# Routing of a mixture-of-experts layer: six tiles of 96 tokens, a scale for each token, and rows added into DRAM by accumulating DMAs

## The chip, the core and the metric

The kernel runs on one core of a Trainium2 chip. The time is that of the device, in microseconds, for one execution of the whole program. Runs before and after are compared by their median. Five engines work side by side: PE (TensorE, matmuls), DVE (VectorE), ACT (ScalarE), POOL (GpSimd) and SP (SyncE, which here only issues DMAs).

## The reference

One inference step of a decoder of two layers on 576 tokens (512 of a new sequence, 64 of eight others) with 1024 channels. Each layer has a mixer of three branches (S5, attention over a paged cache, Mamba-2) with an output projection w_o. Layer 0 goes on with a dense SwiGLU, layer 1 with eight experts, of which each token uses two. Around the end of layer 1's mixer, where the change lies, it computes:

```python
x = layer_norm(ALPHA * x + m, ln1_g[1], ln1_b[1])        # m: mixer's output, behind w_o
logits = x @ w_router + b_router                          # 576 x 8
top_val, top_idx = lax.top_k(logits, 2)
top_w = softmax(top_val)
f = sum over e of gate[:, e] * (silu(x @ w_gate[e]) * (x @ w_up[e])) @ w_down[e]
x = layer_norm(ALPHA * x + f, ln2_g[1], ln2_b[1])
```

## The kernel before

Activations lie with channels on the 128 partitions and tokens along the free axis, in eight blocks of channels, and tokens in two halves of 288 (`HF`, `h` = 0 and 1). Matmuls run with 32-bit operands that are split into a high and a low part: each weight block (512 KB, loaded by SP in `wload`, L265) is split into `wh` by ACT (L97) and `wl` by DVE (L106) in `wsplit`; three matmuls (L294 to L296) make one product. TensorE runs through weight block after weight block, and the splits are made some blocks ahead.

At the end of layer 1's mixer, `mixer_out` does for each half eight w_o blocks, each followed by an addition of the residual, and then the layer norm in `Norm.finish`: subtract the mean (L1466), squares on ACT (L1468), sums over channels by matmuls with a matrix of ones (L1470), router logits by matmuls of 8 output rows (L1479, tile `lgp`), root (L1481), a reciprocal 288 wide on all partitions (L1482), product with it, then gain and bias on ACT (L1494). With half 0 this lies beside half 1's w_o; with half 1 nothing is left for TensorE to do beside it.

`route` comes once, after half 1, for all 576 tokens in five tiles of 128 (the last 64): logits are transposed to tokens on partitions, the two largest are found, counted (matmuls L1693 to L1695 give each token's position in its expert), and ten matmuls with one-hot rows (`rsel`, L1712 and L1713) turn positions into the list of tokens of each expert's 176 slots (`tl`). Beside it `route_half` transposes the normalised rows and writes them to a DRAM tensor `X1D` by DMAs on ACT's queue (L1661; half 0's also to `X1C`, L1663). The weights of tokens are written to a DRAM table `WT` (L1751, L1752). `overflow` then loads the largest count into registers of all engines and branches (L1862, L1863); its body, for more than 176 tokens in one expert, isn't entered in the runs shown.

The expert loop gathers each expert's rows from `X1D` by two indirect DMAs on POOL (`gather`, L1762 and L1764), transposes and splits them (`tokens`, tile `xe`), runs gate, up and down blocks (`mm2`, L1788 to L1791; silu at L1809), and adds the result rows into `X1C` by two accumulating indirect DMAs (L1854). The slot weights come from `WT` by two indirect gathers for each expert, 16 in all (`slot_weights`, L1757, tile `rsw`).

Elsewhere, `gather_logs` (L972) issues 16 indirect gathers into `lfp` for each layer from POOL at the start of the program; `fox_sample` copies them out (L1001). The tile has two buffers.

Engines take their instructions in program order, and the framework puts in waits where tiles or DRAM tensors depend on each other; `tc.issue_after` orders instructions of one engine.

Of the kernel before, what the change touches and what calls it, by code (L numbers as in the profile page):

```python
# [36 lines left out]
FLAG, SLAG, ZLAG = 3, 1, 1  # L37
NPRE, NPS, NPP = 5, 2, 1
# [7 lines left out]
def decoder_step(ctx, tc, A, O):  # L46
# [79 lines left out]
    def dexp(out, x, n):  # L126
        ki_ = wk.tile([P, 80], I32, name="eki", bufs=1)
        f = wk.tile([P, 3, 80], F32, name="ef", bufs=1)
        k_, a_, r_, p_ = ki_[:, :n], f[:, 0, :n], f[:, 1, :n], f[:, 2, :n]
# [62 lines left out]
    tokid = consts.tile([P, 5], I32, name="tokid")  # L192
    pool.iota(tokid, pattern=[[P, 5]], base=0, channel_multiplier=1)
# [37 lines left out]
    def tr(out, in_, n):  # L231
        pe.transpose(out, in_, ident[:n, :n])  # L232
# [1200 lines left out]
    class Norm:  # L1433
# [19 lines left out]
        def finish(self, pr, g0, b0, ecol, out, mid=None):  # L1453
            R, h = self.R, self.h
            late = mid and h
# [9 lines left out]
            for j in range(8):  # L1465
# [3 lines left out]
                if h:  # L1469
                    last_ = pe.matmul(pv[:, :HF], lhsT=ones, rhs=sq, start=(j == 0), stop=(j == 7))  # L1470
# [6 lines left out]
            with tc.issue_after(last_.ins) if late else nullcontext():  # L1477
                for j in range(8 if mid else 0):
                    pe.matmul(lo_, lhsT=M["wr"][:, j], rhs=R(j), start=(j == 0), stop=(j == 7))  # L1479
# [3 lines left out]
            if mid:  # L1483
                mid(h, lo_, rs)
            for j in range(8):
                if late and j % 2:
                    M["pl"] = mul(pool, R(j), R(j), rs)
                else:
                    mul(dve, R(j), R(j), rs)
                g_, b_ = pr[:, g0 + j:g0 + j + 1], pr[:, b0 + j:b0 + j + 1]  # L1490
                if h and j % 2 and not late:
# [3 lines left out]
                out(j, h, R(j))  # L1495

# [3 lines left out]
    def mixer_out(l, mhl, out, done):  # L1500
# [4 lines left out]
        for h in range(2):  # L1505
# [3 lines left out]
            for j in range(8):  # L1509
# [4 lines left out]
                nrm.ready(j)  # L1514
            nrm.finish(prm[l], R_L1G, R_L1B, 1, out, done and done[0])
            if done:
                done[1](r, h)
# [59 lines left out]
    MB = dict(C=8, M=8, W=2, L=2, RW=2, XS=3, SQ=3, GT=6)  # L1577
# [31 lines left out]
    WT = dr.tile([T * NE, 1], F32, name="WT")  # L1609
# [4 lines left out]
    def route_init():  # L1614
        M["wr"] = U("RW", [P, 8, 8], F32, name="rtw")
        pool.dma_start(out=M["wr"], in_=A["moe_w_router"][0].rearrange("(k p) e -> p k e", p=P))
# [3 lines left out]
        M["rows"] = consts.tile([P, 2, 2, 5], I32, name="rrow")  # L1620
        M["wts"] = consts.tile([P, 2, 2, 5], F32, name="rwt")
# [6 lines left out]
        M["tw"] = consts.tile([P, 2, 8], I32, name="rtw8")  # L1628
        M["sw"] = consts.tile([P, 2, 8], F32, name="rsw")
        M["io"] = io = U("W", [P, CAP], F32, name="io")  # L1630
# [4 lines left out]
    def route_prep():  # L1635
        wb = U("RW", [P, 8, 8], F32, name="rtb")
        mul(dve, wb, M["wr"], bc(prm[1][:, R_L1B:R_L1B + 8], 2, 8))
        mul(dve, M["wr"], M["wr"], bc(prm[1][:, R_L1G:R_L1G + 8], 2, 8))
# [3 lines left out]
        add(dve, M["brt"], M["brt"], pt[:, 0:8])  # L1642

    def route_mid(h, o, rs):
        if not h:
            M["lg"] = wk.tile([P, T], F32, name="lg", tag="xp", bufs=4)
        mul(dve, M["lg"][:8, HS[h]], o, rs[:8])
        if h:
            route()

    def route_half(r, h):
        for i in ((0, 1), (2, 3, 4))[h]:
            n = P if i < 4 else 64
            t_ = U("C", [P, D], name="x1t")
            for j0 in (0, 4):
                pt = PF()
                for j in range(4):
                    k = j0 + j
                    tr(pt[:n, j * P:(j + 1) * P], r[k // 2][:, k % 2, i * P:i * P + n], P)
                M["x1"] = cp(t_[:n, j0 * P:j0 * P + 512], pt[:n])  # L1660
            act.dma_start(out=X1D[i * P:i * P + n], in_=t_[:n])  # L1661
            if h == 0:
                act.dma_start(out=X1C[i * P:i * P + n], in_=t_[:n])  # L1663

    def route():
        sc = U("C", [P, 640], name="rsc")
        pt = PX()
        L = sc[:, 0:40].rearrange("p (a b) -> p a b", a=5)
        dve.memset(L, 0.0)
        for i in range(5):  # L1670
            n = P if i < 4 else 64
            tr(pt[:n, i * 8:(i + 1) * 8], M["lg"][:8, i * P:i * P + n], 8)
        add(dve, L[:, 0:4], pt[:, 0:32].rearrange("p (i e) -> p i e", i=4), bc(M["brt"], 1, 4))
        add(dve, L[:64, 4], pt[:64, 32:40], M["brt"][:64])
        mx = sc[:, 40:80].rearrange("p (a b) -> p a b", a=5)
        ix = sc[:, 80:120].bitcast(U32).rearrange("p (a b) -> p a b", a=5)
        for i in range(5):
            dve.max(mx[:, i], L[:, i])
            dve.max_index(ix[:, i], mx[:, i], L[:, i])
        ef = sc[:, 120:130].rearrange("p (a b) -> p a b", a=2)  # L1680
        dve.tensor_copy(ef, ix[:, :, 0:2].rearrange("p i c -> p c i"))
        oh = sc[:, 130:210].rearrange("p (a b c) -> p a b c", a=2, b=5)
        for c in range(2):
            dve.tensor_tensor(oh[:, c], bc(e8f, 1, 5), bc(ef[:, c], 2, 8), op=OP.is_equal)
            dve.memset(oh[64:, c, 4], 0.0)
        cnt = sc[:, 210:250].rearrange("p (a b) -> p a b", a=5)
        add(dve, cnt, oh[:, 0], oh[:, 1])
        ls = sc[:, 250:298].rearrange("p (a b) -> p a b", a=6)
        dve.memset(ls[:, 0], 0.0)
        for i in range(5):  # L1690
            add(dve, ls[:, i + 1], ls[:, i], cnt[:, i])
        pt = PX()
        pe.matmul(pt[:, :40], lhsT=bef, rhs=cnt, start=True, stop=False)  # L1693
        pe.matmul(pt[:, :40], lhsT=ones, rhs=ls[:, 0:5], start=False, stop=True)
        pe.matmul(pt[:, 64:72], lhsT=ones, rhs=ls[:, 5], start=True, stop=True)  # L1695
        tmp = sc[:, 298:378].rearrange("p (a b c) -> p a b c", a=2, b=5)
        rp = sc[:, 378:388].rearrange("p (a b) -> p a b", a=2)
        for c in range(2):
            mul(dve, tmp[:, c], pt[:, :40].rearrange("p (i e) -> p i e", i=5), oh[:, c])
        dve.tensor_reduce(rp.rearrange("p c i -> p (c i)"), tmp.rearrange("p c i e -> p (c i) e"), axis=AX.X, op=OP.add)  # L1700
        oht = U("W", [P, 2, 5, 8], F32R, name="oht")
        tokf = sc[:, 420:425]
        dve.tensor_scalar(tokf, tokid, 1.0, None, op0=OP.add)
        for c in range(2):
            mul(dve, oht[:, c], oh[:, c], bc(tokf, 2, 8))
        io = M["io"]
        pl = PX()
        n_ = 0
        for c in range(2):
            for i in range(5):  # L1710
                s_ = wk.tile([P, CAP], F32R, name="rsel", tag="h288", bufs=4)
                (dve, dve)[i % 2].tensor_scalar(s_, io, rp[:, c, i:i + 1], None, op0=OP.is_equal)  # L1712
                pe.matmul(pl[:8, 0:CAP], lhsT=oht[:, c, i], rhs=s_, start=(n_ == 0), stop=(n_ == 9))  # L1713
                n_ += 1
        ps_ = sc[:8, 440:440 + CAP]
        dve.tensor_copy(ps_, pl[:8, 0:CAP])
# [321 lines left out]
```

## Time and profile before

| what | value |
|---|---|
| timed runs | 2384.43, 2384.25, 2366.11 us |
| median | 2384.25 us |
| profiled execution, its own time | 2400.34 us |
| its span in the trace | 2398.7 us |
| PE busy | 2277.4 us (95%) |
| DVE, ACT, POOL busy | 66%, 47%, 23% |
| mean granted clock of TensorE | 0.968 of full speed |

The span is the trace's first to last instruction; 1.6 us lie around it. Busy time is what instructions of an engine cover; a high share says that the engine bounds the kernel on the whole, not in each stretch. In the rows below a start is in microseconds from the start of the span, the number in brackets is the idle time ahead of the instruction, and behind the arrow stands what ended it ("issue": nothing that the profile shows).

### The profile page before, as it was taken

What the parts mean: (1) busy time and instruction counts of PE and PEld (TensorE: products, weight loads), DVE (VectorE), ACT (ScalarE), POOL (GpSimd) and SP (SyncE); (2) the same over time, 40 slices, a digit from 0 to 9 for tenths busy, and PEclk for the clock granted to TensorE, in tenths of its full rate; (3) what the DMA queues carried; (4) which work ended last, traced back from release to release, by engine and by line L of the source; (5) the groups of instructions that cost most, each with busy time, mean ns of one, the idle gap of its engine ahead of it and who ended that gap; (6) DMA issues with size and microseconds to landing.
All of it is one profiled execution on the core that took longest, in us unless ns stands there. A gap on an engine that the chain in (4) does not pass through costs nothing. (4 is left out here: it accounts for less than half of the span.)

```text
span 2398.7 us, 45369 instructions
## 1 busy us (share of the span) xinstructions
PE 2277.4 (95%) x17037; PEld 2158.2 (90%) x17038; DVE 1573.7 (66%) x3725; ACT 1134.5 (47%) x2538; POOL 560.4 (23%) x712
## 2 busy tenths in 40 slices
PE   5999999998999999999999999899999699999995
PEld 5899997888998999999899998789999599999995
DVE  4956687556588843334765697456447578888886
ACT  2354443453346323223644443354334467777773
POOL 6733224333130110001124324233003310101000
PEclk7999999999999999999999999899999799999997
DMA  5566556856445432233576557757333799999993
GB/s 125 174 177 206 160 155 186 202 160 215 118 126 157 147 96 83 80 89 103 139 188 184 157 152 195 186 156 211 89 99 108 199 229 255 255 253 259 236 258 100
DMA packets 587436, 399.91 MB, mean 167 GB/s; under 512 B 59436, under 2 KB 548188, under 8 KB 587176
## 3 DMA queue, kind: packets, MB, share of 16 engines
q1 hardware_dynamic: 475272, 236.30, 37.2%
q0 software_dynamic: 30912, 95.12, 14.4%
q10 hardware_dynamic: 81024, 65.51, 9.5%
q8 instruction: 136, 2.23, 0.4%
q14 instruction: 92, 0.75, 0.1%
HBM read 326.02 MB, written 70.92 MB: 165 GB/s over the span
## 5 line engine op out<-in xcount | busy, mean ns | idle before, releaser
L106 DVE TENSOR_TENSOR wl<-wr,wh 128x512 fp32r<-128x512 f32 x886 | 629.1, 719 | 364.0 <-ACT wh L97 346.6
L97 ACT ACTIVATE wh<-wr 128x512 fp32r<-128x512 f32 x886 | 549.0, 625 | 511.0 <-PE mm L295 364.9
L294 PE MATMUL mm<-xh,wh 128*128 128x288 f32 (+1 forms) x2048 | 617.8, 302 | 15.3 <-issue 7.9
L295 PE MATMUL mm<-xl,wh 128*128 128x288 f32 (+1 forms) x2048 | 613.9, 300 | 7.9 <-issue 5.2
L296 PE MATMUL mm<-xh,wl 128*128 128x288 f32 (+1 forms) x2048 | 612.8, 299 | 5.1 <-issue 4.4
L294 PEld LDWEIGHTS mm<-xh,wh 128*128 128x128 f32 (+1 forms) x2048 | 386.3, 189 | 26.0 <-issue 11.6
L295 PEld LDWEIGHTS mm<-xl,wh 128*128 128x128 f32 (+1 forms) x2048 | 386.1, 189 | 17.1 <-issue 10.9
L296 PEld LDWEIGHTS mm<-xh,wl 128*128 128x128 f32 (+1 forms) x2048 | 385.8, 188 | 13.1 <-issue 9.8
L1788 PE MATMUL mm<-xe,wh 128*128 128x352 f32 x448 | 134.3, 360 | 1.8 <-issue 1.8
L1788 PE MATMUL pf<-xe,wh 128*128 128x352 f32 x448 | 132.2, 358 | 0.5 <-issue 0.5
L1789 PE MATMUL mm<-xe,wl 128*128 128x176 f32 x512 | 118.0, 251 | 1.8 <-issue 1.8
L1789 PE MATMUL pf<-xe,wl 128*128 128x176 f32 x512 | 117.6, 250 | 1.5 <-issue 1.5
L294 PE MATMUL mm<-hq,wh 128*128 128x288 f32 x352 | 104.3, 296 | 0.2 <-DVE rf L103 0.2
L294 PE MATMUL pf<-xh,wh 128*128 128x288 f32 x352 | 104.3, 296 | 0.0
L296 PE MATMUL mm<-hq,wl 128*128 128x288 f32 x352 | 104.2, 296 | 0.0
L296 PE MATMUL pf<-xh,wl 128*128 128x288 f32 x352 | 104.1, 296 | 0.0
L295 PE MATMUL pf<-xl,wh 128*128 128x288 f32 x352 | 103.8, 295 | 0.0
L295 PE MATMUL mm<-hq,wh 128*128 128x288 f32 x352 | 103.7, 295 | 0.0
L1789 PEld LDWEIGHTS mm<-xe,wl 128*128 128x128 f32 x512 | 97.9, 194 | 1.6 <-issue 1.6
L1789 PEld LDWEIGHTS pf<-xe,wl 128*128 128x128 f32 x512 | 97.2, 193 | 0.5 <-issue 0.5
L1788 PEld LDWEIGHTS mm<-xe,wh 128*128 128x128 f32 x448 | 86.5, 193 | 2.4 <-issue 2.4
L1337 ACT ACTIVATE gt<-mm,prm 128x288 f32<-128x288 f32 x96 | 47.4, 494 | 85.4 <-PE mm L296 75.1
(662 smaller groups left out, 5310.4 us busy)
## 6 DMA issues: line engine op xcount, KB each, us to landing
wr<-in_w_in_dram SPq DMA_DIRECT2D x108, 512.0 KB
wr<-in_moe_w_gate_dram SPq DMA_DIRECT2D x64, 512.0 KB
wr<-in_moe_w_up_dram SPq DMA_DIRECT2D x64, 512.0 KB
wr<-in_moe_w_down_dram SPq DMA_DIRECT2D x64, 512.0 KB
wr<-in_w_o_dram SPq DMA_DIRECT2D x32, 512.0 KB
wr<-in_ffn_w_gate_dram SPq DMA_DIRECT2D x25, 512.0 KB
wr<-in_ffn_w_up_dram SPq DMA_DIRECT2D x25, 512.0 KB
wr<-in_ffn_w_down_dram SPq DMA_DIRECT2D x24, 448.0 KB
```

Source lines behind the costliest of these rows:

```text
L97: return act.activation(out, in_, AF.Copy)
L106: e.tensor_tensor(out, a, b, op=OP.subtract)
L294: pe.matmul(o, lhsT=wh_[:, a, :m], rhs=x[0][:, k, s], start=(st and k == 0), stop=False)
L295: pe.matmul(o, lhsT=wh_[:, a, :m], rhs=x[1][:, k, s], start=False, stop=False)
L296: S["mm"] = pe.matmul(o, lhsT=wl_[:, a, :m], rhs=x[0][:, k, s], start=False, stop=(sp_ and k == kt - 1))
L1337: act.activation(t[h], o[h], AF.Tanh, scale=0.5, bias=prm[l][:, c0:c0 + 1])
L1788: pe.matmul(o, lhsT=h_[:, k % 4, :], rhs=xf, start=(k == 0), stop=False)
L1789: pe.matmul(o[:, 0:CAP], lhsT=l_[:, k % 4, :], rhs=x[:, k, 0], start=False, stop=False, skip_group_check=True)
```

## The change

Tokens are routed in six tiles of 96, three for each half. Half 0's logits, counts and one-hot matmuls (`route_half`, `route_tiles(0)`) are done beside half 1's w_o blocks.

Half 1 gets a function of its own, `finish_tokens`. Logits and sums of squares are each gathered in four groups of 32 output rows, so that a copy and three transposes bring them to tokens on partitions; root and reciprocal are taken of a tile of 96 x 3, and the logits are scaled for each token. Then come `route_tiles(1)` and `route_lists`. The rows of half 1 are made by matmuls of the centred activations with a diagonal matrix of gains (`dg`), scaled per token as ACT moves them out of PSUM, and added to `X1D` by three accumulating indirect DMAs from POOL. The bias is preset: a DMA has written ln1_b into rows 288 to 575 of `X1D` before.

The table `WT`, its two writes and the 16 `rsw` gathers are gone; `slot_table`, behind the If, makes all slot weights by 12 one-hot rows, 12 matmuls and two transposes. The integers for the overflow case are made inside the If (`route_rows`). `lfp` has one buffer in place of two. `M["pl"]` no longer orders the first split of expert weights on POOL, half 0's rows are 0 to 287 rather than 0 to 255, and the copy from `X1D` to `X1C` starts at row 288.

```diff
-        lfps[l] = lfp = wk.tile([P, 16, 8], F32, name="lfp", bufs=2)
+        lfps[l] = lfp = wk.tile([P, 16, 8], F32, name="lfp", bufs=1)
...
+        def finish_tokens(self):
+            R, pm = self.R, self.pm
+            pv, lo = PX(), PA("lgp")
+            for j in range(8):
+                stt(R(j), pm[:, :HF], -1.0 / 1024, R(j), OP.mult, OP.add)
+                sq = U("SQ", [P, HF], F32, name="sq")
+                act.activation(sq, R(j), AF.Square)
+                g = slice(j % 4 * 32, j % 4 * 32 + 32)
+                pe.matmul(lo[g, :HF], lhsT=M["wr"][:, j], rhs=R(j), start=(j < 4), stop=(j >= 4), skip_group_check=True)
+                last_ = pe.matmul(pv[g, :HF], lhsT=ones[:, 0:32], rhs=sq, start=(j < 4), stop=(j >= 4),
+                                  skip_group_check=True)
+            part = []
+            for q, src in enumerate((pv, lo)):
+                t_ = U("L", [P, HF], F32, name="lnt")
+                cp(t_, src[:, :HF]) if q == 0 else dve.tensor_copy(t_, src[:, :HF])
+                pt = PX()
+                for i in range(3):
+                    last_ = tr(pt[:RT, i * P:(i + 1) * P], t_[:, i * RT:(i + 1) * RT], P)
+                part.append(pt[:RT, :3 * P].rearrange("p (i g c) -> p i c g", i=3, g=4))
+            vs, rs = M["vs"], M["rs"]
+            red = M["red"]
+            dve.tensor_reduce(vs, part[0][:, :, 0], axis=AX.X, op=OP.add)
+            act.activation(vs, vs, AF.Sqrt, scale=1.0 / 1024, bias=eps[:RT, 1:2])
+            dve.reciprocal(rs, vs)
+            dve.tensor_reduce(red, part[1][:, :, 0:8], axis=AX.X, op=OP.add)
+            mul(dve, red, red, bc(rs, 2, 8))
+            add(dve, M["L"][:, 3:6], red, bc(M["brt"][:RT], 1, 3))
+            route_tiles(1)
+            route_lists()
+            t_ = [U("M", [P, D], name="x1t") for i in range(3)]
+            for n, (i, j0) in enumerate((i, j0) for i in range(3) for j0 in (0, 4)):
+                pt = (MM, PF)[j0 // 4]()
+                cs = slice(j0 * P, j0 * P + 512)
+                with tc.issue_after((last_ if n < 3 else M["cnm"]).ins):
+                    for j in range(j0, j0 + 4):
+                        pe.matmul(pt[:RT, (j - j0) * P:(j - j0 + 1) * P], lhsT=R(j)[:, i * RT:(i + 1) * RT],
+                                  rhs=M["dg"][j // 2][:, j % 2], start=(j == j0), stop=(j == j0 + 3), skip_group_check=True)
+                M["x1"] = act.activation(t_[i][:RT, cs], pt[:RT], AF.Copy, scale=rs[:, i:i + 1])
+                if j0:
+                    pool.indirect_dma_start(out=X1D, in_=t_[i][:RT], in_offset=None, compute_op=OP.add,
+                                            out_offset=bass.IndirectOffsetOnAxis(ap=tokid[:RT, 3 + i:4 + i], axis=0))
...
+            if done and h:
+                nrm.finish_tokens()
+                continue
...
     def route_prep():
...
+        pool.dma_start(out=X1D[HF:T], in_=A["ln1_b"][1].unsqueeze(0).to_broadcast([HF, D]))
+        M["dg"] = [U("GT", [P, 2, P], name="dg") for q in range(4)]
...
+    def route_tiles(h):
+        ts = slice(3 * h, 3 * h + 3)
...
+        pe.matmul(pt[:RT, :24], lhsT=bef[:RT, :RT], rhs=cnt[:, ts], start=True, stop=False)
+        pe.matmul(pt[:RT, :24], lhsT=ones[:RT, :RT], rhs=ls[:, ts], start=False, stop=True)
+        if h:
+            M["cnm"] = pe.matmul(pt[:RT, 64:72], lhsT=ones[:RT, :RT], rhs=ls[:, NT], start=True, stop=True)
...
+            for i in range(3 * h, 3 * h + 3):
                 s_ = wk.tile([P, CAP], F32R, name="rsel", tag="h288", bufs=4)
...
+                pe.matmul(M["pl"][:8, 0:CAP], lhsT=oht[:RT, c, i], rhs=s_[:RT], start=(h == c == i == 0),
+                          stop=(c == 1 and i == NT - 1))
...
-            act.dma_start(out=wtv[0:512].rearrange("(i p) e -> p i e", p=P), in_=tmp[:, 0, 0:4])
-            act.dma_start(out=wtv[512:T], in_=tmp[:64, 0, 4])
...
+    def slot_table():
+        tmp, wt, ps_ = M["tmp"], route_weights(), M["ps_"]
+        for c in range(2):
+            mul(dve, tmp[:, c], M["oh"][:, c], bc(wt[:, c], 2, 8))
+        pw = P5("pw")
+        for c in range(2):
+            for i in range(NT):
+                s_ = wk.tile([P, CAP], F32, name="rsel", tag="h288", bufs=4)
+                dve.tensor_scalar(s_[:RT], M["io"][:RT], M["rp"][:, c, i:i + 1], None, op0=OP.is_equal)
+                pe.matmul(pw[:8, 0:CAP], lhsT=tmp[:, c, i], rhs=s_[:RT], start=(c == i == 0),
+                          stop=(c == 1 and i == NT - 1))
+        dve.tensor_copy(ps_, pw[:8, 0:CAP])
...
-            pool.indirect_dma_start(out=M["sw"][:CH_, q, e:e + 1], out_offset=None, in_=WT,
-                                    in_offset=bass.IndirectOffsetOnAxis(ap=M["tw"][:CH_, q, e:e + 1], axis=0))
...
         overflow()
         WB["body"] = False
+        slot_table()
...
-                if j == 1 and e < NE - 1:
-                    slot_weights(e + 1)
...
-            if e == 0:
-                slot_weights(0)
```

## Rows read from the trace of the kernel before

**Rows 1.** The page's first part: busy time and share of each engine.
```profile
PE 2277.4 (95%) x17037; PEld 2158.2 (90%) x17038; DVE 1573.7 (66%) x3725; ACT 1134.5 (47%) x2538; POOL 560.4 (23%) x712
```

**Rows 2.** Timeline of TensorE: start, duration, line, operation, count, idle before.
```profile
22.60 0.29 PE L294 MATMUL mm<-xh,wh 128*128 128x288 f32 x1 [1.83 <-issue]
...
1857.94 0.60 PE L232 MATMUL pf<-ident,r 128*128 128x128 f32 x4
...
1861.46 0.29 PE L296 MATMUL mm<-mh,wl 128*128 128x288 f32 x1
...
1882.06 0.43 PE L1695 MATMUL px<-rsc,br 128*128 128x8 f32 x2
...
1899.49 1.43 PE L232 MATMUL px<-ident,g 88*128 88x88 f32 x8 [12.18 <-ACTq L1863]
...
1902.63 0.64 PE L1788 MATMUL mm<-xe,wh 128*128 128x352 f32 x1
```

**Rows 3.** Timeline of ACT around the routing, its DMA issues (ACTq) with it.
```profile
1863.80 3.67 ACT L1468 ACTIVATE sq<-r 128x288 f32<-128x288 f32 x8 [2.33 <-DVE r L109]
...
1885.54 0.46 ACTq L1661 DMA_DIRECT2D X1D<-x1t  x1
...
1891.92 0.53 ACTq L1752 DMA_DIRECT2D WT<-rsc  x1
1899.60 1.28 ACT L97 ACT_TABLE_LOAD   x1 [13.05 <-ACTq L1863]
```

**Rows 4.** Timeline of DVE around the routing.
```profile
1869.43 1.95 DVE L1482 RECIPROCAL rs<-rs 128x288 f32<-128x288 f32 x1 [3.18 <-ACT rs L1481]
...
1887.45 0.15 DVE L1722 COPY tl<-px 88x2 f32<-88x2 f32 x1
```

**Rows 5.** Timeline of POOL from the first row gather on, accumulates with it.
```profile
1890.11 1.06 POOL L1762 DMA_INDIRECT g<-X1D,rtl  x1 [11.05 <-DVE ef L109]
...
1902.17 1.02 POOL L1757 DMA_INDIRECT rsw<-WT,rtw  x1 [9.11 <-DVE xe L106]
...
1924.06 0.98 POOL L1757 DMA_INDIRECT rsw<-WT,rtw  x1 [0.31 <-issue]
...
1983.43 1.69 POOL L1854 DMA_INDIRECT X1C<-y,rts  x1 [8.69 <-ACT eg L97]
1992.19 2.02 POOL L1854 DMA_INDIRECT X1C<-y,rts  x1 [7.07 <-DVE eg L103]
...
2149.72 1.66 POOL L1854 DMA_INDIRECT X1C<-y,rts  x1 [8.67 <-ACT eg L97]
2159.76 1.61 POOL L1854 DMA_INDIRECT X1C<-y,rts  x1 [8.37 <-DVE wl L106]
```

**Rows 6.** Stretches: length, busy time of PE, PEld, DVE, ACT, POOL, clock, DMA.
```profile
20.50:39.50 19.00, 2.97 (x10) 2.10 (x8) 0.00 (x0) 0.00 (x0) 11.99 (x13) 0.60 0.27 53
...
500.00:530.00 30.00, 30.00 (x291) 25.57 (x295) 13.56 (x34) 15.79 (x36) 9.61 (x11) 1.00 0.47 131
...
1840.00:1861.60 21.60, 21.60 (x159) 20.91 (x158) 12.93 (x28) 12.42 (x21) 0.67 (x1) 1.00 0.21 74
...
1917.90:1927.00 9.10, 3.58 (x14) 2.64 (x14) 1.94 (x5) 1.24 (x4) 5.61 (x6) 0.74 0.87 202
```

**Rows 7.** Timeline of ACT: the first silu of experts 0, 1 and 2.
```profile
1913.81 0.35 ACT L1809 ACTIVATE eg<-eg 128x176 f32<-128x176 f32 x1
...
1977.55 0.34 ACT L1809 ACTIVATE eg<-eg 128x176 f32<-128x176 f32 x1
...
2033.00 0.34 ACT L1809 ACTIVATE eg<-eg 128x176 f32<-128x176 f32 x1
```

**Rows 8.** Timeline of POOL at the start: the first and the last of 24 gathers.
```profile
5.72 1.12 POOL L972 DMA_INDIRECT lfp<-in_cache_logf_dram,pgi  x1 [0.39 <-POOL lms L986]
...
35.20 0.95 POOL L972 DMA_INDIRECT lfp<-in_cache_logf_dram,pgi  x1 [0.31 <-issue]
```

**Rows 9.** Timeline of DVE: the last copies out of layer 0's lfp.
```profile
507.96 1.04 DVE L1001 COPY lq<-lfp 128x64 f32<-128x64 f32 x4
```

More of the change, by code (lines that the diff above doesn't have):

```diff
@@ L231, in tr @@
     def tr(out, in_, n):
-        pe.transpose(out, in_, ident[:n, :n])
+        return pe.transpose(out, in_, ident[:n, :n])
     xts = {}
@@ L1469, in finish @@
                 if h:
-                    last_ = pe.matmul(pv[:, :HF], lhsT=ones, rhs=sq, start=(j == 0), stop=(j == 7))
+                    pe.matmul(pv[:, :HF], lhsT=ones, rhs=sq, start=(j == 0), stop=(j == 7))
                 elif j == 0:
@@ L1476, in finish @@
                 pe.matmul(pv[:, :HF], lhsT=ones, rhs=s2, start=True, stop=True)
-            with tc.issue_after(last_.ins) if late else nullcontext():
-                for j in range(8 if mid else 0):
-                    pe.matmul(lo_, lhsT=M["wr"][:, j], rhs=R(j), start=(j == 0), stop=(j == 7))
+            for j in range(8 if mid else 0):
+                pe.matmul(lo_, lhsT=M["wr"][:, j, 0:8], rhs=R(j), start=(j == 0), stop=(j == 7))
             rs = U("SQ", [P, HF], F32, name="rs")
@@ L1483, in finish @@
             if mid:
-                mid(h, lo_, rs)
+                mid(lo_, rs)
             for j in range(8):
[L1486 to L1489, printed above, removed]
+                mul(dve, R(j), R(j), rs)
                 g_, b_ = pr[:, g0 + j:g0 + j + 1], pr[:, b0 + j:b0 + j + 1]
-                if h and j % 2 and not late:
+                if h and j % 2:
                     dve.tensor_scalar(R(j), R(j), g_, b_, op0=OP.mult, op1=OP.add)
@@ L1658, in route_half @@
                     k = j0 + j
[L1659 to L1677, printed above, removed]
+                    tr(pt[:RT, j * P:(j + 1) * P], r[k // 2][:, k % 2, ts], P)
@@ L1688, in route @@
-        ls = sc[:, 250:298].rearrange("p (a b) -> p a b", a=6)
-        dve.memset(ls[:, 0], 0.0)
-        for i in range(5):
+            dve.tensor_tensor(oh[:, c, ts], bc(e8f[:RT], 1, 3), bc(ef[:, c, ts], 2, 8), op=OP.is_equal)
+        add(dve, cnt[:, ts], oh[:, 0, ts], oh[:, 1, ts])
+        for i in range(3 * h, 3 * h + 3):
             add(dve, ls[:, i + 1], ls[:, i], cnt[:, i])
         pt = PX()
-        pe.matmul(pt[:, :40], lhsT=bef, rhs=cnt, start=True, stop=False)
-        pe.matmul(pt[:, :40], lhsT=ones, rhs=ls[:, 0:5], start=False, stop=True)
@@ L1867, in overflow @@
             pool.dma_start(out=TL.rearrange("(p c) o -> p (c o)", p=P), in_=z)
+            n = RT
             for c in range(2):
-                for i in range(5):
-                    n = P if i < 4 else 64
+                for i in range(NT):
                     off = bass.IndirectOffsetOnAxis(ap=M["rows"][:n, 0, c, i:i + 1], axis=0)
@@ L1886, in overflow @@
                                (YO, e * (NOV * CAP) + c * CAP))
-            for i in range(5):
-                n = P if i < 4 else 64
+            for i in range(NT):
                 xt = U("CX", [P, D], name="cx")
-                sp.dma_start(out=xt[:n], in_=X1D[i * P:i * P + n])
+                sp.dma_start(out=xt[:n], in_=X1D[i * n:(i + 1) * n])
                 for c in range(2):
```

167 lines of the change are left out of this document (86 added, 81 removed).

## Prediction

> **What bounds the kernel now.** I read the page's first part, then busy time by stretches, then the timeline of each engine around the change, each with the question what TensorE waits for. TensorE is busy for 95% of the span [rows 1], so only two things can move the time: work added to TensorE, and the few places where it stands still. Three of those are touched here. *The routing bubble:* the last w_o matmul of layer 1 starts at 1861.46 and ends 0.29 later; the first expert matmul starts at 1902.63 [rows 2], 40.9 us with little real work for TensorE. In it the chain is: centring and squares on ACT [rows 3], a 1.95 us reciprocal 288 wide and the list of slots, ready at 1887.45 [rows 4], the count matmul at 1882.06 [rows 2], the last row write X1D issued at 1885.54 [rows 3], the first gather of expert rows at 1890.11 [rows 5], the WT writes on ACT until 1891.92 [rows 3], and then a wait of 12.18 us that ends at 1899.49 [rows 2]. Its releaser is the branch of the overflow If on ACT's queue, not the gather. After that ACT loads a table, 1.28 us [rows 3]. *The stall of expert 0:* in the stretch 1917.9 to 1927.0 TensorE works 3.58 of 9.10 us, and DVE and ACT stop with it [rows 6], while GpSimd issues the rsw gathers, an unbroken run from 1902.17 to 1924.06 (17 indirect issues, two of them row gathers) [rows 5]. Expert 0 takes 63.74 us from silu to silu, expert 1 takes 55.45 [rows 7]: 8.3 us too many. *The stall at the start:* GpSimd issues 24 lfp gathers in one run, 5.72 to 35.20 [rows 8]; from 20.5 to 39.5 TensorE works 2.97 of 19.00 us, DVE and ACT nothing, DMA is at 0.27 [rows 6], and the gaps between matmuls, as the one ahead of 22.60, have no releaser in the profile [rows 2]. Both stalls begin about 12 issues into a run. I have no row for why; I treat it as what long runs of indirect DMAs do in this kernel.
>
> **The change part by part**, against the profiled execution (2400.34 us; 16.1 above the median of the timed runs, 2384.25, and 34.2 above the lowest, 2366.11).
>
> *(a) lfp with one buffer.* Only layer 0's 16 gathers can be issued at the start; layer 1's need the buffer that the last lq copy of layer 0 frees at about 508 [rows 9]. With a pitch of 29.48/23 = 1.28 us, a run of 16 ends about 8 x 1.28 = 10.3 us earlier, and the stall with it: 19.0 becomes some 8.4 us long. Taken −10.6; ends 0 (the stall isn't there when nothing records) and −19 (16 don't trigger it).
>
> *(b) The 16 moved gathers* are issued after 508. TensorE is busy all of 500 to 530 with 9.61 us of GpSimd work in it [rows 6]: GpSimd issues other DMAs there that break the run, and the data isn't needed for hundreds of us. Taken 0; up to +8.4 if they go out as one run of 16. Queued behind them on GpSimd are the page gathers of layer 0; if those wait, TensorE does.
>
> *(c) Half 0's routing moves under half 1's w_o.* There TensorE is busy 21.60 of 21.60 us [rows 6], so each of its added instructions counts in full: a third 96-token tile gives 8 more transposes at 0.60/4 = 0.15, as in the row at 1857.94 [rows 2], 1.2; six one-hot matmuls at the 0.43/2 = 0.22 of the small matmul at 1882.06 [rows 2], 1.3; three count matmuls, 0.7; three transposes of logits, 0.4. Sum +3.6 (2 to 6). DVE is busy 12.93 of those 21.60 us [rows 6] and takes some 5.5 more; it hides as long as the weight splits on the same engine come in time. If they don't, TensorE waits for wl, and that is the 6.
>
> *(d) When the gather can start.* Two things must be there, the list and the rows in DRAM. The list: half 0's part is done early, the 288-wide reciprocal becomes one of 96 x 3, and half the tiles remain. The 10.7 us from that reciprocal's end (1871.38, [rows 4]) to the count matmul (1882.06, [rows 2]) should halve; with the per-token scale at about 1870 (squares end at 1863.80 + 3.67 = 1867.5 [rows 3], then a copy, three transposes, a sum, a root) the count comes at about 1875.3 and the list at 1878, 9 us before the 1887.45 of now. But this gain is not on the path: the rows come last. The first tile's add can start at about 1873.0 (scale at 1870, two evictions at about 0.6, issue). The second and third have matmul groups ordered behind the count and are ready at about 1877 and 1878.6. The three adds go into one DRAM tensor, by indices that nothing compares, so I expect each to wait until the one before has landed, as the pairs into X1C do. The gather follows the third. The trace has no accumulate on a quiet DMA. Near rows: a plain write, issued at 1885.54 [rows 3], lets the gather go at 1890.11 [rows 5], 4.6 us; pairs of accumulates, 1.69 + 7.07 = 8.8 us apart, up to 1.66 + 8.37 = 10.0 (seven pairs in all) [rows 5], but beside full weight traffic, which the stretch of routing has not. Neither row is nearer; I take the middle of 4.6 and 8.8, 6.7: 1873.0 + 3 x 6.7 = 1893.1, +3.0 against 1890.11. Ends: 4.6 gives −3.3, 10.0 gives +12.9.
>
> The Trainium skill, "DMA: Bandwidth & Descriptors", section "Anatomy of one DMA — SWDGE (gpsimd) path", fits a DMA of this path as 2.0 us plus bytes at 436 GB/s; for a tile of 96 x 1024 floats that is an estimate of 2.9 us. The pairs at 8.8 speak against it; by it the gather would go at the third tile's 1878.6 + 2.9 (the fourth rival).
>
> *(e) From gather to first matmul*, now 1902.63 − 1890.11 = 12.5. The WT writes are gone from ACT, so ACT passes the If while the adds run, and its table load (1.28) falls into the wait: −1.3 surely. Further, TensorE would begin when the gathered rows land, not at the branch: two gathers (second 1.36 behind) and 4.6 to land give 1896.1 instead of 1899.49, up to −3.4. I take half of that: −3.0 in all (−1.3 to −4.7). The new slot table (12 one-hot rows on DVE, 12 small matmuls, some 8 us of DVE) stands in the wait for the gathered rows; if the wait is short it costs up to 3, since xe's evictions on DVE are queued behind it.
>
> *(f) The rsw gathers go*, and with them the run in which expert 0 stalled: −8.3 [rows 7] (0 to −8.3).
>
> Sum: −10.6 + 0 + 3.6 + 3.0 − 3.0 − 8.3 = **−15.3**; profiled about 2385. The median of the timed runs is 18.1 above the lowest, which is the size of one stall (19.0 − 2.97 = 16.0, or both in part), so I take it that the timed runs of 2384 have most of the stall at the start too: 2384.25 − 15.3 = 2369. The same from below: 2366.11 without stalls plus c, d, e = +3.6 gives 2369.7. So **2369**. One per cent is 24 us, and a measurement of this kernel can't tell less than that from no change.
>
> **The rivals.** *First, the stalls belong to the recorded run alone.* They have no releaser, and the profiled run is 16 above the median; then only c, d, e count: 2384.25 + 3.6 = 2388. Against it: the spread of the timed runs has just that size. 0.25. *Second, slower: the three adds in a row.* If each takes the busy pitch of 8.8 to 10.0, the gather waits until 1903.0, +12.9; with c and e that is +13.5, and, without credit for stalls, 2398. It costs time from a pitch of (1890.11 − 0.6 − 1873.0)/3 = 5.5 us on; if the stalls really go (−18.9), only from 11.8 on. For it: seven pairs, all at 8.8 or more. Against: there the DMA engines are full. 0.10. *Third, the adds don't wait for each other.* Then the third, ready at 1878.6, lands at 1885.3 and the gather goes 4.8 earlier than now: −15.3 − 7.8, 2361. The early list gets its worth. 0.07. *Fourth, the adds are short* as by the fit: the gather at 1881.7, 8.4 earlier, −15.3 − 11.4, 2358. 0.06. That the change doesn't do what it says is in the forecast itself: the list comes 9 us earlier and nobody is waiting for it.
>
> **How the numbers follow.** Forecast 2369: 0.52. 2388: 0.25; 2398: 0.10; 2361: 0.07; 2358: 0.06. The range 2355 to 2395 takes in all but the second rival and the outer ends of c and d. Faster by over 1% is under 2360.4: the fourth rival, half of the third, and a little of the forecast's lower part, 0.13. Slower by over 1% is over 2408: the second rival with splits late or a third stall, 0.04. The rest, 0.83, is within 1%.
>
> **What would show it.** Right: at the start the gaps of TensorE end at about 27 to 30; no stretch like 1917.9 to 1927.0, and all experts at 55.5 us from silu to silu; three X1D adds on GpSimd 6 to 7 us apart with nothing but the one before to wait for, and the first gather some 31 us after the last w_o matmul begins; ACT past the If before the gather is issued. Wrong in (d): adds 9 us apart, or back to back. Wrong in (b): a stretch near 510 in which all engines stand still while GpSimd issues lfp gathers. Wrong in (c): w_o of half 1 longer by more than 6 us with TensorE waiting for wl. What would make the prediction wrong as a whole: the timed runs not having the stalls (2388), or a new stall somewhere else of the same kind.

## Result and the profile after

The changed kernel takes 2401.76 us (median of four runs, 2399.71 to 2408.11), the kernel before 2384.34 beside it: ratio 1.0095, interval 1.0066 to 1.0125. (A ratio here is taken over all single runs; that of the two medians would be 1.0073, since one of the four runs before took 2366.) I had forecast 2369. It is slower by 17 us where a gain of 15 was forecast. The set of runs matters here: beside the experiments the kernel before took 2399, 2402, 2378 and 2405 us, each set on another chip, and the changed kernel, run in two of those sets, came out at 1.0052 (1.0026 to 1.0077) and 1.0042 (1.0027 to 1.0056). It was slower each time, by 9 to 17 us in the medians.

Its profiled execution takes 2402.18 us (span 2400.5), that of before 2400.34. Two spans that are almost alike hide gains and losses of 5 to 15 us each. I find them by comparing the time at which SP issues the same weight block in both traces; the lag is the changed kernel's time less the other's.

| weight block | before | after | lag | what lies ahead of it |
|---|---|---|---|---|
| 17th | 123.82 | 118.73 | −5.09 | start |
| 57th | 524.46 | 518.62 | −5.84 | most of layer 0's mixer |
| 73rd | 606.68 | 615.23 | +8.55 | the moved lfp gathers |
| 281st | 1834.84 | 1841.74 | +6.90 | dense layer, layer 1's mixer |
| 313th | 1963.97 | 1962.72 | −1.25 | routing bubble and expert 0 |
| end of span | 2398.7 | 2400.5 | +1.8 | the other experts and the end |

Busy time of the engines, which answers to [rows 1]:

```profile
PE 2281.0 (95%) x17105; PEld 2160.7 (90%) x17106; DVE 1565.8 (65%) x3753; ACT 1131.0 (47%) x2533; POOL 541.4 (23%) x697
```

Busy time by stretches of the changed kernel; the columns are those of [rows 6].

```profile
10.00:20.50 10.50, 4.89 (x21) 4.30 (x20) 4.70 (x8) 3.47 (x7) 7.81 (x9) 0.62 0.83 214
60.00:120.00 60.00, 51.65 (x367) 49.74 (x367) 49.46 (x95) 16.25 (x32) 39.92 (x39) 0.89 0.57 166
505.00:530.00 25.00, 23.75 (x176) 21.89 (x175) 13.20 (x26) 10.00 (x20) 19.11 (x18) 1.00 0.56 159
530.00:560.00 30.00, 27.90 (x284) 25.49 (x285) 9.55 (x21) 6.41 (x14) 7.69 (x12) 0.94 0.59 180
560.00:640.00 80.00, 67.03 (x464) 65.06 (x463) 49.91 (x93) 31.92 (x60) 24.95 (x43) 0.91 0.52 158
```

In 505 to 640 TensorE works 118.7 of 135 us; in the kernel before it works 127.9, and does so without a gap up to 560 ([rows 6] has 500 to 530). That is 9.2 us of the 14.4 by which the lag grows from the 57th to the 73rd block. The rest goes along with a lower granted clock: 0.94 and 0.91 in the last two stretches, against 1.00 and 0.94 before. GpSimd is busy 19.11 of the first 25 us, against 8.22 before. The timeline of GpSimd tells with what:

```profile
508.04 1.21 POOL L973 DMA_INDIRECT lfp<-in_cache_logf_dram,pgi  x1 [0.92 <-issue]
...
526.44 0.96 POOL L973 DMA_INDIRECT lfp<-in_cache_logf_dram,pgi  x1 [0.30 <-issue]
527.70 0.95 POOL L1012 DMA_INDIRECT kpg<-in_cache_k_dram,pgi  x1 [0.30 <-issue]
...
531.45 0.94 POOL L973 DMA_INDIRECT lfp<-in_cache_logf_dram,pgi  x1 [0.30 <-issue]
...
542.24 1.01 POOL L1038 DMA_INDIRECT vpg<-in_cache_v_dram,pgi  x1 [1.56 <-PE pa L1034]
...
1882.09 1.59 POOL L1532 DMA_INDIRECT X1D<-x1t,tokid  x1 [3.28 <-ACT x1t L1530]
1888.28 1.59 POOL L1532 DMA_INDIRECT X1D<-x1t,tokid  x1 [4.61 <-DMA X1D<-x1t,tokid]
1894.56 1.42 POOL L1532 DMA_INDIRECT X1D<-x1t,tokid  x1 [4.69 <-DMA X1D<-x1t,tokid]
1900.63 1.02 POOL L1810 DMA_INDIRECT g<-X1D,rtl  x1 [4.65 <-DVE rsel L1790]
```

As soon as layer 0's last copy has freed the one buffer, 14 lfp gathers go out in a row, then two page gathers of layer 0 (kpg), then the last two. In the kernel before the two kpg go at 514.26 and the next vpg at 527.82; here at 527.70 and 542.24. TensorE waits for just that, and longer than before for the gates and sums that have slipped with it (waits of TensorE from 505 to 640: total, times, longest):

```profile
PE px L1264 <- POOL lns L104: 5.5, 1, 5.5
PE mm L295 <- DVE gt L110: 5.0, 3, 3.6
PE px L233 <- DMA kpg<-in_cache_k_dram,pgi: 3.3, 1, 3.3
PE mm L295 <- ACT gt L1338: 2.4, 1, 2.4
```

These are 16.2 us; the kernel before has 7.0 in the same stretch:

```profile
PE px L1263 <- POOL lns L103: 4.1, 1, 4.1
PE mm L294 <- DVE gt L109: 2.9, 1, 2.9
```

At the end of the routing the timeline of GpSimd shows three adds 6.2 and 6.3 us apart, each waiting for the one before to land, and the gather 6.1 behind the third. (For the gather the profile names a one-hot row of the slot table, rsel, which it doesn't read; by its distance I take the wait for the third add's landing.) TensorE around it, which answers to [rows 2]:

```profile
14.92 0.61 PE L295 MATMUL mm<-xh,wh 128*128 128x288 f32 x1 [4.49 <-ACT wh L98]
...
1870.44 0.30 PE L297 MATMUL mm<-mh,wl 128*128 128x288 f32 x1
...
1896.21 5.68 PE L1791 MATMUL pw<-rsel,lms 96*8 96x176 f32 x24 [9.22 <-DVE lms L101]
...
1905.38 0.38 PE L233 MATMUL px<-ident,g 88*128 88x88 f32 x1 [2.75 <-DMA g<-X1D,rtl]
1907.81 1.29 PE L233 MATMUL px<-ident,g 88*128 88x88 f32 x7 [2.06 <-DMA g<-X1D,rtl]
...
1910.25 0.64 PE L1836 MATMUL mm<-xe,wh 128*128 128x352 f32 x1
```

From the end of the last w_o matmul to the first expert matmul it is 39.5 us, against 40.9 [rows 2]. What ends the wait is now the gathered rows, no longer the branch. The slot table's matmuls (1896.21 to 1901.9) lie in it and cost nothing. From the first expert matmul to expert 1's first silu it was 1977.55 − 1902.63 = 74.9 us [rows 2, 7]; now expert 1's silu is at

```profile
1976.28 0.34 ACT L1857 ACTIVATE eg<-eg 128x176 f32<-128x176 f32 x1
```

which makes 66.0: the stall of expert 0 is gone.

### The profile page after: what moved, and what is told of

It reads as the page before. It is cut to its first block, busy times and chain, and to the rows that moved or that the text cites. A ratio compares the mean times of both kernels' runs of the same rounds, so it can differ in the third digit from the quotient of the medians.

```text
span 2400.5 us, 45495 instructions
## 1 busy us (share of the span) xinstructions
PE 2281.0 (95%) x17105; PEld 2160.7 (90%) x17106; DVE 1565.8 (65%) x3753; ACT 1131.0 (47%) x2533; POOL 541.4 (23%) x697
## 5 line engine op out<-in xcount | busy, mean ns | idle before, releaser
L295 PEld LDWEIGHTS mm<-xh,wh 128*128 128x128 f32 (+1 forms) x2048 | 388.2, 190 | 23.5 <-ACT wh L98 10.6
```

The source lines that it names most:

```text
L295: pe.matmul(o, lhsT=wh_[:, a, :m], rhs=x[0][:, k, s], start=(st and k == 0), stop=False)
```

## Experiments

Each set of runs has its own chip and its own runs of the kernel before; ratios are to those, intervals 95%. A run of gathers, below, means gathers issued one behind the other with nothing between; a gap without a releaser is idle time of TensorE that the profile puts to nothing ("issue"). Theory A says that the single lfp buffer makes the loss, by the place to which it moves layer 1's gathers. The rivals are the routing itself and the preset of X1D at the start.

### Set 1: the buffer, the preset, one part at a time (before: 2399.26)

**Late gathers.** Edit on the changed kernel: layer 1's gathers are ordered behind a sum in layer 0's w_o, at about 700 us.

```diff
-                    add(pool, s2, s2, sq)
+                    lfps["o"] = pool.tensor_tensor(s2, s2, sq, op=OP.add)
...
-        gather_logs(1)
+        with tc.issue_after(lfps["o"].ins):
+            gather_logs(1)
```

> The changed kernel, but layer 1's 16 lfp gathers are ordered behind the last square sum of layer 0's w_o half 0 (about 700 us) and no longer stand ahead of page gathers at 508 to 531. Theory: in the changed kernel these 16 issues hold up layer 0's page gathers (kpg, vpg) and GD reads on GpSimd by some 13 us, and TensorE loses 14 us between 520 and 620; so this version takes 2402 - 14 = 2388 us. Rival: the loss of the changed kernel comes from the routing with its adds and from the start, and TensorE waits in 520 to 620 for something else; then 2402, within 3 us. If a run of 16 issues makes all engines stall, some 8 us reappear near 700: 2396.

Measured: 2397.64, ratio 0.998 (0.9953 to 1.0007). The loss goes. At the new place (719.50 to 740) the run of 16 brings something back: TensorE has gaps without a releaser of 6.3 us there, and works 22.04 of the 30 us from 730 to 760.

**Late bias.** Edit: the preset of X1D goes out behind the load of the router weights.

```diff
-        pool.dma_start(out=M["wr"][:, :, 0:8], in_=A["moe_w_router"][0].rearrange("(k p) e -> p k e", p=P))
+        M["wrd"] = pool.dma_start(out=M["wr"][:, :, 0:8], in_=A["moe_w_router"][0].rearrange("(k p) e -> p k e", p=P))
...
-        pool.dma_start(out=X1D[HF:T], in_=A["ln1_b"][1].unsqueeze(0).to_broadcast([HF, D]))
+        with tc.issue_after(M["wrd"].ins):
+            pool.dma_start(out=X1D[HF:T], in_=A["ln1_b"][1].unsqueeze(0).to_broadcast([HF, D]))
```

> The changed kernel, but the DMA that presets 1152 KB of X1D with the bias goes out behind the load of router weights (about 1650 us) and not at 4 us. Theory: at 4 us it shares the DMA engines with the first token rows and weights, and TensorE's first matmul block waits 4.5 and 1.1 us for its split weights; without it 5 to 6 us less, 2396. Rival: those loads are late for their own reasons and the start is bound by later work on DVE; then 2402, within 3 us.

Measured: 2419.56, ratio 1.0089 (1.0059 to 1.0118). No gain. At the start of this trace the wait for the first split weights has gone, but gaps without a releaser (7.3 us) and waits for wl (6.8) stand in its place: with a run of 16 gathers beside it the preset is not what holds TensorE up last. The preset is tried again below, without the run.

**Two buffers.** Edit: `bufs=2` for lfp again; the slot weights' tile moves to the expert phase's pool to make room.

> The changed kernel with lfp in two buffers as before (the slot weights' tile moves to the expert phase's pool to make room). Theory that the wait at 520 to 620 is the moved gathers: 2388 if the long run of gathers at the start costs timed runs nothing; 2404 if the stall of some 16 us at the start of the recorded run of before is in timed runs too. Rival that the moved gathers are harmless: 2402 without, 2418 with the stall.

Measured: 2415.93, ratio 1.006 (1.0036 to 1.0084). This run doesn't decide, since the edit did something else as well. The place behind 508 is mended (the lag grows by 1.4 us over it), but the routing has a new wait, in the list of TensorE's waits from 1860 to 1945:

```profile
PE pw L1790 <- DVE lms L101: 33.1, 1, 33.1
```

9.2 in the changed kernel: the first expert weights are loaded some 29 us later (1899.56 against 1870.81), and DVE's splits of them stand ahead of the slot table. I take it that the moved tile shifted the weight buffers onto space that is freed late; this I haven't tested.

**One buffer in the kernel before.** Edit: `bufs=1` for lfp, nothing else.

> The kernel before with one buffer for lfp, nothing else changed. Theory: the moved gathers alone cost 14 us behind 508; at the start the run shortens from 24 to 16 issues. If the stall at the start is no part of timed runs: 2384 + 14 = 2398. If it is: 2384 - 16 + 14 = 2382. Rival, moved gathers harmless: 2384 or 2368.

Measured: 2427.40, ratio 1.0105 (1.0071 to 1.0139): 28 us for one number. So the buffer alone makes a loss as large as the whole change; whether the rest of the change gives something back needs both in one set (set 4). Its lag to the kernel before is −3.3 us at 335 and +30.6 at 607, and from 524 to 538 its trace has gaps without a releaser of 10.6 us.

### Set 2: runs of gathers broken up (before: 2401.86)

**The changed kernel again.**

> The changed kernel itself, beside the others on one chip. One buffer for lfp alone cost 1.05% there (2427 against 2399). Theory that the buffer is the whole loss: the rest of the change is worth little, as the version with late gathers was at 0.998; so 1.007 to 1.012, 2416 to 2428. Rival, that the loss is the routing's as well: over 1.012.

Measured: 2416.99, ratio 1.0052. A little below the bounds of the theory: the rest of the change seems to be worth more than I had put it.

**Groups.** Edit on the changed kernel: no run longer than a few gathers. Layer 0's go four by four behind the four writes of u, layer 1's two by two behind the sums of layer 0's w_o.

```diff
-    def gather_logs(l):
+    def gather_logs(l, behind):
...
+            with tc.issue_after(behind[min(i // 2, len(behind) - 1)].ins):
...
-        gather_logs(1)
+        gather_logs(1, lfps["s"])
```

> The changed kernel with the lfp gathers broken up: layer 0's 16 go out four by four behind the four writes of u, layer 1's two by two behind the sums of layer 0's w_o, so that no run of indirect DMAs is longer than 8. Theory: in every trace so far in which 12 or more indirect DMAs go out in a row, TensorE, DVE and ACT stand still for 6 to 16 us from about the twelfth on; without runs these stalls go at both places, some 9 at the start and 6 at 700 against the version with late gathers (2397.6): 2383, ratio 0.993. Rival, the stall hangs on something else in those stretches and comes back: 2398.

Measured: 2384.26, ratio 0.991 (0.9879 to 0.994), as the theory says: 33 us below the changed kernel. In its trace there are no gaps without a releaser at the start or around 700. What I had written of "every trace so far" was too much: the changed kernel's first trace has two runs of 16 and no such gap.

**Groups in the kernel before.** The same edit on the old kernel, two buffers.

> The kernel before (two buffers, old routing, 16 rsw gathers) with the lfp gathers broken up in the same way. Theory of runs: its stall of 16 us at the start goes, the one of expert 0 (run of rsw gathers) stays: 2399 - 12 = 2387, ratio 0.995. It should stay behind the changed kernel with groups by the stall of expert 0 and the shorter bubble, 5 to 10 us. Rival, that the new routing is worth nothing: the two versions with groups are level within 3 us.

Measured: 2380.56, ratio 0.9916 (0.9886 to 0.9946). The intervals lie on each other: the rival, level, stands. With the runs broken up no difference between the old routing and the new is seen.

**Groups, plain writes.** Edit: ACT's eviction, then the bias added on GpSimd, then a plain DMA; no preset, no accumulate; slot table behind expert 0's transposes.

```diff
+                add(pool, t_[i][:RT, cs], t_[i][:RT, cs], M["b1"][:RT, cs])
                 if j0:
-                    pool.indirect_dma_start(out=X1D, in_=t_[i][:RT], in_offset=None, compute_op=OP.add,
-                                            out_offset=bass.IndirectOffsetOnAxis(ap=tokid[:RT, 3 + i:4 + i], axis=0))
+                    act.dma_start(out=X1D[HF + i * RT:HF + (i + 1) * RT], in_=t_[i][:RT])
```

> The changed kernel with groups, and half 1's rows written by plain DMAs from ACT: the bias is added on GpSimd to the row tiles, nothing is preset, nothing accumulates; the slot table comes behind the transposes of expert 0's rows. Theory that three adds in a row set the gather's start (1882.1, 1888.3, 1894.6, gather at 1900.6): the last row tile is ready at 1886 + 1.2 for the bias, a plain write takes 4.6, so the gather goes at about 1892 and the first expert matmul 8 us earlier: 2375, 8 below the version with groups. Rival, the wait is only moved, onto the slot table or the bias adds on GpSimd: within 3 us of the version with groups.

Measured: 2374.74, ratio 0.99 (0.9852 to 0.9947): not told from the version with groups. In its trace the bubble is 35.1 us in place of 39.3 and the gather goes 25.3 behind the last w_o matmul, not 21; expert 0 gives 2.7 back (silu to silu 54.7 against 52.0). It isn't shown why: the version with DVE's bias below has the slot table in the same place, and 52.0. The rest of the gain in the bubble is lost on DVE while GpSimd adds: the list of slots is ready 22.7 us behind the last w_o matmul, in place of 16.4. From GpSimd's timeline:

```profile
1852.62 3.78 POOL L104 TENSOR_TENSOR x1t<-x1t,b 96x512 f32<-96x512 f32 x3 [2.29 <-ACT x1t L1530]
```

and from DVE's in the same stretch:

```profile
1853.96 1.22 DVE L101 TENSOR_TENSOR oht<-lms 96x24 fp32r<-96x24 f32 x1
1855.11 0.17 DVE L104 TENSOR_TENSOR lms<-lms 96x24 f32<-96x24 f32 x1
1855.20 1.24 DVE L101 TENSOR_TENSOR oht<-lms 96x24 fp32r<-96x24 f32 x1
```

The same instruction takes 0.18 in the changed kernel; here 1.22, which is one GpSimd add (1.26). The Trainium skill, "SBUF — State Buffer", section "Terms", says that of DVE and GpSimd one holds their shared port pair for a full instruction and that the loser blocks fully. These rows agree.

### Set 3: which routing, when nothing stalls (before: 2377.66)

**Groups and late preset.**

> The changed kernel with groups, and the preset of X1D sent behind the load of router weights (about 1650 us). In the profile of the version with groups alone TensorE waits 7.5 us for the first split weights; in the two versions with groups and without a preset at the start it waits 1.7. Theory: the preset of 1152 KB at 4 us costs 6 us at the start, which the stall covered when it was moved alone: ratio to before 0.991 - 0.0025 = 0.9885, 6 us below the version with groups. Rival: the difference at the start is that of two schedules; 0.991.

Edit: groups, and the late preset of set 1. Measured: 2374.31, ratio 0.9983 (0.9966 to 0.9999). Both numbers expected were ratios to a kernel before that takes 2400; in this set it takes 2378, so neither can be told from the other by them.

**Groups, bias added by DVE.**

> As the version with groups and plain writes, but the bias is added by VectorE as it moves the rows out of PSUM (one instruction for scale and bias), not by GpSimd afterwards. In that version DVE instructions took up to 1.2 us in place of 0.2 while GpSimd added, and the gather went 25.5 us behind the last w_o matmul (30.0 with three adds). Theory: without that the gather goes at about 22 and the first expert matmul at 32, 3 us below the version with GpSimd's adds: ratio 0.988 to 0.989. Rival: DVE's own six evictions of 0.7 us push the list of slots back by as much; no gain, 0.990.

Edit: as the plain writes, but one DVE instruction (`scalar_tensor_tensor`, times rs plus bias) moves the rows out of PSUM. Measured: 2377.91, ratio 1.0002 (0.9984 to 1.002). No gain. Here the list of slots is ready only at 1867.05, the last row eviction on DVE at 1865.6, and the gather goes 26.8 behind the last w_o matmul. But the edit did something else as well, so the rival isn't shown. The first splits of expert weights were ordered behind `M["x1"]`, the last row eviction, which was an instruction of ACT and is now one of DVE. ACT now splits two weight blocks in the middle of the squares (the trace has a wh split at 1849.23, with five of the eight squares behind it), and the logits come 13.4 us behind the last w_o matmul, not 9.3, ahead of the first eviction. That is 4.1 of the 8.0 us by which the list is late; the six evictions of 0.74 among the steps of the routing can have no more than the other 3.9.

**Groups in the kernel before, again.**

> The kernel before with groups once more, beside the two others on one chip. Theory from the traces: the new routing gains 0.7 us in the bubble and 5.4 at expert 0 and pays 1.8 under w_o and some 6 for the preset at the start; with the preset moved it should be 4 to 6 us ahead, so 0.991 here against 0.9885 there. Rival: level within 2 us.

Measured: 2376.99, ratio 0.9997 (0.9978 to 1.0016). In this set the kernel before itself takes 2378, so breaking up its runs brings nothing here, where it brought 21 us in set 2. So the timed runs of the kernel before had the stall of long runs in set 2 and hardly in set 3; in sets 1 and 4, where it takes 2399 and 2405, I take it to be there too. The sets ran on different chips; whether the chip makes the difference isn't tested. As the kernel before varies so, ratios of different sets can't be set side by side. Within set 3 the new routing with a late preset stands 2.7 us ahead of the old (intervals overlap). For the preset at the start the traces show this, first groups alone, then with the late preset (TensorE's waits from 5 to 60):

```profile
PE mm L295 <- ACT wh L98: 7.5, 2, 5.9
```

```profile
PE mm L295 <- ACT wh L98: 1.7, 2, 1.2
```

That is 5.8 us at that place, but other waits take most of it over: with the late preset TensorE waits 6.7 us for DVE (brn) and 3.7 for a DMA (prow), where it waited 6.3 for token rows. All its waits from 5 to 60 come to 14.1 and 12.1 us, and by 335 us the two traces are level (lags of −13.0 and −12.9 at the 41st block). So the preset at the start isn't shown to cost anything.

### Set 4: dividing the loss (before: 2405.10)

**The changed kernel, third time.**

> The changed kernel once more. The kernel before took 2384, 2399, 2402 and 2378 on four chips, while the versions with groups took 2374 to 2384 on all: so the stall at the start is there in part of the chips' runs. Theory: the changed kernel has its loss (gathers ahead of page gathers behind 508) on every chip, and the kernel before has its stall only on some; so on a chip where before takes 2378 to 2386 this is 17 to 30 slower, where before takes 2399 it is 12 to 17 slower. Rival: both have the same stalls; level where before is fast.

Measured: 2414.42, ratio 1.0042 (1.0027 to 1.0056), 9.3 us slower: a little less than the theory's 12 to 17. TensorE waits in 505 to 640 of this trace:

```profile
PE mm L295 <- issue: 9.3, 1, 9.3
PE mm L295 <- DVE gt L110: 7.6, 4, 3.6
PE px L1264 <- POOL lns L104: 5.5, 1, 5.5
PE mm L295 <- ACT gt L1338: 1.8, 2, 1.6
```

**One buffer in the kernel before, again.**

> The kernel before with one buffer for lfp, again, now beside the changed kernel. Theory: the buffer is the whole loss, so this is at least as slow as the changed kernel: ratio 1.005 to 1.012. Rival: part of the loss is the routing; then 1.000 to 1.004 and clearly below the changed kernel.

Measured: 2428.09, ratio 1.0089 (1.0063 to 1.0116). One buffer costs 23.0 here; with the rest of the change on top of it, 13.7 come back.

**Groups for layer 1 alone.**

> The changed kernel with only layer 1's lfp gathers broken up, two by two behind the sums of layer 0's w_o; layer 0's go out at the start in one run of 16, beside the preset. Theory: the loss behind 508 goes whole, and nothing comes at 700; what is left against the version with all groups (0.991 where before took 2402) is the start: 8 to 10 us above it, so 2385 to 2392. Rival: breaking up the start was the gain, and this is as slow as the changed kernel.

Edit: as groups, for layer 1's gathers only. Measured: 2391.36, ratio 0.9942 (0.9923 to 0.9961): 23.1 below the changed kernel, by layer 1's 16 gathers alone. One stretch of the changed kernel of this set, and the same of this version:

```profile
530.00:560.00 30.00, 17.50 (x106) 16.91 (x105) 7.66 (x15) 4.79 (x9) 11.04 (x13) 0.72 0.45 133
```

```profile
530.00:560.00 30.00, 29.98 (x312) 27.55 (x311) 13.43 (x29) 7.52 (x16) 4.78 (x9) 1.00 0.66 201
```

12.5 us of waiting in one, none in the other. The granted clock (the column behind GpSimd's) is 0.72 in the first and 1.00 in the second: in the gap of 9.3 us it fell to the lower of its two levels, 1.2 GHz, and stayed there for a while behind it. From the 49th to the 73rd block the first trace falls back by 21.7 us, the second by 0.2. Both lose some 7.5 us ahead of that, between 335 and 455, beside a granted clock of 0.89 (0.96 in the kernel before); as both have it, it isn't the moved gathers.

## Why the prediction was wrong

**The step that failed is (b)**, the 16 moved gathers: "taken 0; up to +8.4 if they go out as one run of 16". They did go out as one run, and they cost 23 us (changed kernel less the version with layer 1's groups; 23 and 28 by the buffer alone). I had written down both halves of it. The run I priced at up to 8.4 and took at 0, because GpSimd's other DMAs would break it; the page gathers queued behind I didn't price. GpSimd's other DMAs didn't break the run: 14 of the 16 stand ahead of the next page gather in GpSimd's order. And what is queued behind them does matter: 14 issues of about 1.3 us put the page gathers 13.4 us later by the clock, 18.3 behind a stream that was running 4.9 ahead, and TensorE ran out of work. That part is in the first trace of the changed kernel (14.4 us of lag between the 57th and the 73rd block, 9.2 of it as longer waits, with not one gap without a releaser). In the trace of set 4 the stall of a long run comes on top of it (9.3 us), and the lag over the same stretch is 14.0, or 21.7 when it is taken from the 49th block on, ahead of the run. "TensorE is busy all of 500 to 530 with 9.61 us of GpSimd work" said that TensorE had work; it didn't say that GpSimd's queue had 20 us to spare before that work ran out.

Alone, 23 us on (b) would have made 2392. The rest of the miss lies in (a) and the base. With the sizes found for the terms (a) to (f), −5 to 0, 23, 1.8, 1.5, −2.9 and −8.9 (each worked out here or below), the sum is +9.5 to +14.5 where −15.3 was forecast; measured were +17.4, +15.1 and +9.3 in the three sets that had the changed kernel.

**(a)** was right in kind and too large. In the first trace a run of 16 at the start shows no gap without a releaser, and the lag at the 9th block is −15.45. But 10.4 are given back by the 17th: TensorE waits for kz on DVE (5.1) and wl (3.7). In the traces of sets 2 and 4 the 16 do stall, and nothing is left at 335 (+0.4 and +0.1). Forecast −10.6, found −5 to 0. (By its own pitch, 8 × 1.28, the term would be −10.3; nothing hangs on that.)

**A term that I left out** is the preset of X1D. I took it to go where the code has it, in layer 1; it is free to go from the beginning and went at 4.0 us, between the first tokens and weights. In the traces with a late preset the wait of 4.49 us ahead of 14.92 is gone or short, but other waits have come in its place, and no time shows what the preset costs.

**(c)** was +3.6; the w_o stage of layer 1 takes 64.2 us in place of 62.4, +1.8: mis-sized by half. DVE's cover held: TensorE didn't wait for wl there.

**(d)** and **(e)** were right in mechanism, and in size with some luck: the 6.7 was the middle of two far rows, and of (e)'s further gain I had taken half. The adds wait for each other, 6.2 and 6.3 apart and 6.1 to the gather (I took 6.7); the first starts 11.4 us behind the end of the last w_o matmul (11.2 forecast), the gather 29.9 against 28.4 before: +1.5 for +3.0. From gather to first matmul it is 9.6: −2.9 for −3.0; the rows land 7.1 us behind the first gather's issue, where I had 6.0. The estimate of 2.9 us for an add (the fourth rival) is not borne out by these three. That the list comes 9 us earlier and that this is worth nothing was right: it is there at 1887.12, 16.4 behind the last w_o matmul, against 25.7 before, and the rows are what is waited for.

**(f)** was right: −8.3 forecast, 74.9 − 66.0 = 8.9 found.

**The base** was half right. That the stall at the start is in some timed runs and not in others is now shown (the kernel before with groups gains 21 us in set 2 and nothing in set 3), so neither "the stalls belong to the recorded run alone" nor my reading of the spread holds in all sets. For the pair that I forecast the spread was misread, it seems: the two profiles are 1.8 us apart and the medians 17.4, since the recorded execution of the kernel before stands 16.0 above its own median and that of the changed kernel 0.4 above its own. I took stalls off a time that most likely had few of them; as no execution of it near 2384 has a trace, that isn't shown. Nor is it so that less than 1% can't be told from no change: the interval of the result is 0.3% to either side. Taken by itself, the new routing's terms (c to f) come to −8.5 by the rows of the two profiles (1.8 + 1.5 − 2.9 − 8.9), and set 4 has 13.7 for the whole rest of the change, part of which lies in stalls that differ; but with runs broken up in both kernels the two routings are level (sets 2 and 3), and in their traces expert 0 of the old one loses less (silu to silu 57.4 and 54.0, not 63.7), though its run of rsw gathers was left as it was; why isn't known.

The versions with groups took 2374 to 2384 in sets 2 and 3. They are 0.8 to 1% faster in set 2, where the kernel before stalls, and level or nearly so in set 3, where it doesn't; only the old kernel with groups ran in both.

## What to carry to other kernels

A buffer that is taken away is a change to an instruction queue: ask at which moment the freed buffer lets the next writer go, what that queue holds at that moment, and how long the work behind it can wait, before anything is called free. Look in the same way at each new DMA with no inputs, which may go at the very start. In this kernel indirect DMAs were best sent a few at a time between other work; a row of sixteen cost more than a whole rewritten routing gave back. And an edit that moves an instruction to another engine drops the order that others had behind it.

## What the runs showed of the hardware

Beside long runs of indirect DMAs on GpSimd (16 and more) TensorE had gaps that no semaphore explains, in nine traces: at the start in all of them (16.0 us of idle time in the kernel before), near 530 in five (7.9 to 10.8, the largest in the kernel before with one buffer) and at 740 in one (6.3). Not every run has one: the changed kernel's first trace shows none in two runs of 16. In the six traces with groups none was seen at these places. In the start's gaps of the kernel before the engines don't stop altogether: TensorE's matmuls start 2.1 or 2.8 us apart and SP's DMA issues mostly 0.7 or 1.4. What they lack there stays open, and so does whether the recording takes part in it.

An accumulating indirect DMA of 96 rows of 4 KB let what waited for it go after 6.1 to 6.3 us with a DMA share of 0.50 beside it; the pairs into X1C, 88 rows, took 8.8 to 10.0 with a share of 1.07 to 1.16 [rows 5]. Behind a plain write the gather went after 4.6 us in the kernel before and after 3.8 in the version with plain writes.
